# Decoder layer on one core: an SBUF tile moved into a pad, the last relu tiles placed in the u tiles, two down fetches on another queue, other tiles for the DMA adds

## The chip, the cores and the metric

The kernel runs on one core of a Trainium2 chip. A core has a matrix engine (TensorE, PE in the profile), a vector engine (VectorE, DVE), a scalar engine (ScalarE, ACT), GpSimd (POOL) and SyncE (SP). ACT, POOL and SP can each put DMA transfers in a queue of their own; every engine works through its instructions in program order and waits at semaphores. The metric is device time in microseconds; lower is better.

## The reference

One decoder layer, batch 1, 256 tokens, width 2048, all in float32:

```python
h   = rmsnorm(x, norm_attn_pre);  proj = h @ w_in          # 2048 x 4160
A   = dilated sliding-window attention, 8 heads x 128 (q, k, v from proj)
B   = latent attention, 8 heads (c_q @ w_uq, c_kv @ w_ukv, shared rotary key)
x   = x + rmsnorm(concat(A, B) @ w_out, norm_attn_post)    # 2048 x 2048
h   = rmsnorm(x, norm_mlp_pre)
u   = square(relu(h @ w_up))                               # 2048 x 8192
x   = x + rmsnorm(u @ w_down, norm_mlp_post)               # 8192 x 2048
```

## The kernel before

**Three passes.** Every float32 operand of a projection is split into a high part (ACT: a copy rounded to fp32r, line 311, or with a gain column, line 315) and a low part (DVE: value minus high part, lines 312 and 316). A product is then three fp32r matmuls, hi·hi, hi·lo and lo·hi (`three`, line 1083; all matmuls are recorded at line 301). The stationary operand is 128 tokens of the activation (xT, mixT, cqT, hT, u), the moving one up to 512 columns of a weight tile.

**Weights.** `Weights` streams the weights. SP loads a `raw` tile of 128 x 1024 (five buffers), ACT and DVE make `hi` and `lo` of it (eight buffers each), and `get` has tiles emitted six ahead of PE's use. What `weights.first[i]` holds is emitted just before tile i.

**Stages.** Input projections and attention; w_out; the up stage, chunk j = 0 to 7 of 1024 columns of w_up; the down stage, half c = 0 and c = 1 of 1024 columns of w_down, each over 64 row tiles k. Four k share one u tile g = k // 4.

**Pairs by seven products.** A pair of row tiles (2kp, 2kp + 1), with two blocks of 128 tokens and two halves of 512 columns, is a 2 x 2 x 2 block product. For the pairs in `DOWN_SEVEN[c]` (and three pairs in each up chunk but the first) it is done with seven block products in place of eight (`seven_products`, line 1088). For that, one fetch of 1 MB brings both weight tiles (`load_two`, line 378), DVE makes two sums of them (lines 366 to 371), and sums of the left operand are made and split (`st` in the up stage, `four_sums`, line 1040, and `s` tiles in the down stage). A fetch and its sums stand two weight tiles before the pair's first (`SUMS_AHEAD`). In the down stage the fetches alternate between the tile `ab_down` and the tile `c` (c = 0) or `u01` (c = 1), and all are issued by POOL. The products with sums go to accumulators m (up) and md (down); md is allocated at the first pair of a half. Left sums of pairs in both halves are written out (`keep_s`) and fetched back in c = 1.

**From up to down.** For each of u's 16 column tiles j of 512 and each token block b, `up_evac` (line 945) has ACT apply relu and square into a tile `r` (three buffers) and write it to DRAM (`rkeep`, by ACT's queue); 12 us later in the planner's time `turn_u` reloads it in another order (`x` or `c`, line 965, ACT's queue), and 8 us after that DVE transposes it in blocks into `uT[j]` (line 974). The tiles of u14 and u15 have the tag "T", two buffers that the sums of the up pairs used before. Planner's time is a clock that `Flow` advances by 0.216 us with every matmul of 512 columns it emits; it sets the order of the instructions only.

**Low parts of u.** `split_u` makes hi and lo of a u tile. For the tiles in `AWAY` the low part is made without DVE: ACT writes the negated high part to DRAM (`lo_away`, line 988), POOL issues two DMAs that add u to it (line 1000), and the sum is loaded as the low part (`load_lo`, line 1030, POOL). The adds of tiles 10 and up wait until the down stage has begun in the planner's time (`LATE`). The other low parts are written out in c = 0 (`keep_u`, SP's queue), and all but the first are loaded in c = 1.

**Addresses.** The allocator places tiles in steps of 32 bytes of a partition, from the left end (con, wp, then lat or hp, then dp) and from the right end (mix, pa, pb, up). Starts, in bytes of a partition:

| tiles | pool, side | start | remainder at 512 |
|---|---|---|---|
| con_pad, then the small tiles, pwn among them | con, left | 16512 | 128 |
| raw, hi, lo (weights) | wp, left | 18432 | 0 |
| hT_hi, hT_lo | hp, left | 104448, 120832 | 0 |
| ab_down, uhi, ulo, s | dp, left | 104448 and on | 0 |
| xT_hi, xT_lo | pa, right | 116704, 133088 | 480 |
| cqT | pb, right | 123872, 127968 | 480 |
| mixT_hi, mixT_lo | mix, right | 174560, 190944 | 480 |
| st, ab, ab2, c, u01, T, r, uT2 to uT9 | up, right | 139232 and on | 480 |

Slices of 128 tokens or 512 columns of a tile begin at multiples of 512 bytes. In the second half, the low parts of u tiles 4, 7, 8, 11, 12 and 15 lie in the up pool (line 1022).

Of the kernel before, what the change touches and what calls it, by code (L numbers as in the profile page):

```python
# [18 lines left out]
F32 = mybir.dt.float32  # L19
# [7 lines left out]
P = 128  # L27
D = 2048
S = 256
NB = S // P  # L30
# [15 lines left out]
CW = 1024  # L46
# [59 lines left out]
def up_steps(first, *groups):  # L106
    steps = [("k", k) for k in first]
    for i, ks in enumerate(groups):
# [8 lines left out]
N_SEVEN = [sum(w == "w" for w, _ in steps) for steps in UP_STEPS]  # L117


DOWN_SEVEN = ((9, 11, 13, 15, 19, 21, 23, 25, 27, 29), range(3, 28, 2))  # L120
AWAY = range(5, 14, 2)
LATE = 10
SHARED = [k for k in DOWN_SEVEN[0] if k in DOWN_SEVEN[1]]
GT = FF // 512
DOWN_STEPS = [[s for kp in range(2 * GT)
               for s in ([("w", kp)] if kp in ws else [("k", 2 * kp), ("k", 2 * kp + 1)])] for ws in DOWN_SEVEN]

# [141 lines left out]
def layer(nc, tc, io):  # L269
    flow = Flow()  # L270

    def pool(name, side, **kw):
        return tc.alloc_tile_pool(name=name, bufs=1, side=side, **kw)

    con = pool("con", "left")
    con.tile([P, 32], F32, name="con_pad")
    wp = pool("wp", "left")
    ps = tc.alloc_tile_pool(name="ps", bufs=1, space=PSUM)
    dram = tc.alloc_tile_pool(name="dram", bufs=1, space=bass.MemoryType.DRAM)
# [69 lines left out]
    late = {}  # L349

    def seven(load, targets):

        st, tt, H = {}, nc.vector.tensor_tensor, 512

        def fetch():
            ab = st["ab"] = load()
            st["a"], st["b"] = [ab[:, :CW], ab[:, CW:]] if not isinstance(ab, list) else ab

        def sums():
            ab, a, b = st["ab"], st["a"], st["b"]
            t, u = st["t"], st["u"] = targets()
            if not isinstance(ab, list):
                two = [x.rearrange("p (k n) -> p k n", n=H) for x in (t, ab)]
                tt(out=two[0], in0=two[1][:, 0:2, :], in1=two[1][:, 1:4:2, :], op=OP.add)
            else:
                for x, o in ((a, 0), (b, H)):
                    tt(out=t[:, o:o + H], in0=a[:, o:o + H], in1=x[:, H:], op=OP.add)
            tt(out=u[:, :H], in0=t[:, :H], in1=b[:, H:], op=OP.add)  # L370
            tt(out=u[:, H:], in0=u[:, :H], in1=b[:, :H], op=OP.add)  # L371

        def b11(hi, lo):
            split(hi[:, :H], lo[:, :H], st["a"][:, :H])

        return (fetch, sums), [b11] + [lambda hi, lo, n=n: split(hi, lo, st[n]) for n in "but"]

    def load_two(raw, queue, src):
        queue.dma_start(out=raw.rearrange("p (k n) -> p k n", k=2), in_=src.rearrange("(k p) n -> p k n", p=P))
        return raw  # L380
# [54 lines left out]
    def seven_down(c, kp):  # L435
        def load():

            n = DOWN_SEVEN[c].index(kp)
            raw = dpl["ab"]
            if n % 2:  # L440
                raw = late["u01" if c else "c"]
            return load_two(raw, nc.gpsimd, io["w_down"][2 * kp * P:(2 * kp + 2) * P, c * CW:(c + 1) * CW])

        return seven(load, lambda: [late["st"][:, i * CW:(i + 1) * CW] for i in range(2)])

    dpl, left, skeep, wide_d = {}, {}, {}, []
    for c in range(2):
        wide_d.append([])
        for what, k in DOWN_STEPS[c]:
            if what == "k":  # L450
                ts = [weights.plan(down_weight(c, k), 1, CW)]
            else:
                q, parts_q, back = [lambda c=c, k=k, f=f: f(c, k) for f in (down_sums, down_split, down_back)]
# [232 lines left out]
    for half in range(2):  # L686
        qkv = {}
        for nms in (("qk", "v") if not half else "qkv"):
            accs = [acc for _, _, acc in proj(xT, [ch_a[half, nms]], f"{nms}{half}",
                                              bank_of=at_bank if (half, nms) == (0, "v") else None)]  # L690
            for i, nm in enumerate(nms):
                t = pa.tile([P, NB, 512], F32, tag=nm, name=f"{nm}_{half}")
# [146 lines left out]

    pw, pwi = [con.tile([P, NB], F32, name=n) for n in ("pw", "pwi")]  # L840
    pws = con.tile([P, 4, NB], F32, name="pws")
    pwk, pwn = dram.tile([P, NB], F32, name="pwk"), con.tile([P, NB], F32, name="pwn")
    xkeep = [dram.tile([P, D], F32, name=f"xkeep{b}") for b in range(NB)]

    def by_quarter(rows):
# [69 lines left out]
    for ns in ((0, 1), (2,), (3,)):  # L915
# [4 lines left out]
        for c, b, acc in proj(mixT, [ch_o[n] for n in ns], f"o{ns[0]}", order, heads_done):  # L920
            n = ns[c]
# [20 lines left out]

    uT, ukeep = {}, {}

    def up_evac(j, b, acc, order):

        yield UP_STEP * order
        r = late["up"].tile([P, 512], F32, tag="r", bufs=3, name=f"r{j}_{b}")
        nc.scalar.activation(r, acc, AF.Relu, scale=rstd2[b])
        nc.scalar.activation(r, r, AF.Square)  # L950
        keep = dram.tile([P, 512], F32, name=f"rkeep{j}_{b}")
        nc.scalar.dma_start(out=keep.rearrange("(a t) (q c) -> (t q) a c", a=4, q=4),
                            in_=r.rearrange("m (a c) -> m a c", a=4))
        flow.start(turn_u(j, b, keep), D_BACK + (8.0 if (j, b) == (GT - 1, NB - 1) else 0.0))
# [3 lines left out]
    def turn_u(j, b, keep):  # L958

        o = 2 * b + j % 2  # L960
        if j < GT - 2:
            x = closing()[o]
        else:
            x = late["up"].tile([P, 512], F32, tag="r", bufs=3, name=f"x{j}_{b}")
        nc.scalar.dma_start(out=x, in_=keep)
        yield D_TURN
        if j not in uT:
            if j in (0, 1, 10, 11, 12, 13):
                t2 = late["u01" if j < 2 else "ab2" if j < 12 else "ab"][:, j % 2 * CW:(j % 2 + 1) * CW]
            else:  # L970
                tag = {"tag": "T", "bufs": 2} if j > 13 else {"tag": f"uT{j}", "bufs": 1}
                t2 = late["up"].tile([P, CW], F32, name=f"uT{j}", **tag)
            uT[j] = t2.rearrange("p (k s) -> p k s", k=4)
        nc.vector.transpose(uT[j][:, :, b * P:(b + 1) * P].rearrange("p k (q t) -> p k q t", q=4),
                            x.rearrange("p (q k c) -> p k q c", q=4, k=4))
        if b:
            turned.add(j)
            if j in AWAY:
                flow.start(lo_away(j), D_NEG)

    def lo_away(g):

        ukeep[g] = dram.tile([P, CW], F32, name=f"ukeep{g}")
        u = uT[g].rearrange("p k s -> p (k s)")
        for h in range(2):
            c = slice(h * 512, (h + 1) * 512)
            t = late["up"].tile([P, 512], F32, tag="r", bufs=3, name=f"neg{g}_{h}")
            nc.scalar.activation(t.bitcast(F32R), u[:, c], AF.Copy, scale=-1.0)
            yield 1.0
            nc.scalar.dma_start(out=ukeep[g][:, c], in_=t)  # L990
            yield D_LO
        if g < LATE:
            yield D_ADD
        else:
            while not dpl:
                yield 2.0
            yield 4.0 + 5.0 * (g % 2) + 20.0 * ((g - LATE) // 2)
        for h in range(2):
            c = slice(h * 512, (h + 1) * 512)
            nc.gpsimd.dma_start(out=ukeep[g][:, c], in_=u[:, c], accum_op=OP.add)  # L1000
            yield 2.0 if g < LATE else 10.0

    def split_u(c, g):
# [7 lines left out]
        u, h, l = [x.rearrange("p k s -> p (k s)") for x in (uT[g], uh, ul)]  # L1011
        if c and g or g in AWAY:
            nc.scalar.activation(h, u, AF.Copy)
# [18 lines left out]
    def keep_u(g):  # L1032
        ukeep[g] = dram.tile([P, CW], F32, name=f"ukeep{g}")
        nc.sync.dma_start(out=ukeep[g], in_=us[0, g][1].rearrange("p k s -> p (k s)").bitcast(F32))
# [78 lines left out]
    def closing():  # L1113
        return [late["c"][:, i * 512:(i + 1) * 512] for i in range(4)]
# [3 lines left out]
    for j in range(FF // CW):  # L1118
# [9 lines left out]
        for t, b in order:  # L1128
            what, k, tiles = steps[t]
# [14 lines left out]
            if what == "k":  # L1144
                w = weights.get(tiles[0])
                h_done(k, b)
                for n in range(2):
                    c = slice(n * 512, (n + 1) * 512)
                    three(accs[b, n], [tok(hT[x], k, b) for x in range(2)], [w[x][:, 0, c] for x in range(2)], t == 0, t == len(steps) - 1)
                    if j == 0 and t == len(steps) - 1:  # L1150
                        evac.append(flow.start(up_evac(n, b, accs[b, n], 0.75 * (2 * b + n))))
                    flow.pump()
                if b == NB - 1:
                    weights.free(tiles[0])
                continue
# [21 lines left out]
    up = late["up"]  # L1177
# [88 lines left out]
    for c in range(2):  # L1266
# [3 lines left out]
        accs = {(b, n): y[b][2 * c + n] for b, n in PARTS}  # L1270
        ws = DOWN_SEVEN[c]
        for t, (what, k, tiles) in enumerate(wide_d[c]):
            g = (2 * k if what == "w" else k) // 4
# [26 lines left out]
            if nxt not in us:  # L1300
                if not c and g > 1 and g - 1 not in AWAY:
                    keep_u(g - 1)
# [16 lines left out]
    for g in (GT - 2, GT - 1):  # L1319
        for b, n in PARTS:  # L1320
            for kk in range(4):
                k = 4 * g + kk
# [62 lines left out]
```

## Time and profile before

| | us |
|---|---|
| median of 3 runs | 1047.66 |
| lowest, highest | 1044.74, 1049.71 |
| the profiled execution | 1050.24 |
| its span, first to last instruction | 1048.5 |

The profile is of one execution. A row of the groups has line, engine, operation, out<-in, count, busy us, mean ns of one, and the idle time before them with what ended it. Matmul rows overlap each other (390 ns each at a distance of some 230), so the time of a run of matmuls is read from their starts. Half of the transfers' time is SP's queue:

```
q1 hardware_dynamic: 65200, 173.05, 49.9%
q0 software_dynamic: 16656, 59.78, 17.4%
q10 hardware_dynamic: 23376, 19.78, 5.8%
```

(q1 is SP's, q0 POOL's and q10 ACT's queue: packets, MB, share of 16 DMA engines.) The input stages run to about 359 us, the up stage to 699, the down stage to the end.

### The profile page before, as it was taken

To read this page: it belongs to the slowest core of one execution; us is meant where nothing else is said; L and a number is where in the kernel's file an instruction comes from. 1 tells how busy PE (TensorE), PEld (TensorE's weight loads), DVE (VectorE), ACT (ScalarE), POOL (GpSimd) and SP (SyncE) were. 2 spreads that over 40 slices of the span, in tenths; PEclk is the share of its full clock that TensorE was granted. 3 is DMA by queue.
4 is the path that set the end of the run, shared out by engine and by line. 5 is a ranking of instruction groups with operands and counts; after the bars stand their busy time and mean duration, and the time that the engine had idled before them with its cause. 6 is when DMAs were issued, how large, how long until landed. Compare 5 with 4: busy or idle time off the path is not lost.

```text
span 1048.5 us, 13268 instructions
## 1 busy us (share of the span) xinstructions
PE 1035.0 (99%) x4718; PEld 853.5 (81%) x4718; DVE 834.7 (80%) x1125; ACT 634.7 (61%) x850; POOL 64.1 (6%) x102
## 2 busy tenths in 40 slices
PE   9999999999999999999999999999999999999996
PEld 6888889889888878888888888887888888888885
DVE  6675536567547579999999999895899999998786
ACT  6674436556446467666676776675565666766561
POOL 0000000000001010000010100000101000211100
PEclk9999999999999999999999999998999999999999
DMA  8975547454437478877889878789869868888972
GB/s 293 371 221 152 139 131 224 149 163 148 144 130 240 140 287 286 265 243 226 275 253 306 274 225 290 214 280 333 286 243 354 294 211 316 290 306 301 318 267 81
DMA packets 105298, 253.44 MB, mean 242 GB/s; under 512 B 8720, under 2 KB 29712, under 8 KB 104848
## 3 DMA queue, kind: packets, MB, share of 16 engines
q1 hardware_dynamic: 65200, 173.05, 49.9%
q0 software_dynamic: 16656, 59.78, 17.4%
q10 hardware_dynamic: 23376, 19.78, 5.8%
q8 instruction: 37, 0.61, 0.2%
q14 instruction: 29, 0.24, 0.1%
HBM read 224.78 MB, written 27.79 MB: 241 GB/s over the span
## 4 chain that ended last, share of the span: by engine, by line
PE 76%; DVE 10%; issue 6%; DMA 5%; ACT 2%; POOL 1%; ACTq 0%; DVEq 0%; POOLq 0%; SPq 0%
PE acc_u L301 22%; PE y L301 13%; PE acc_o L301 8%; PE m L301 5%; PE acc_qk L301 4%; DVE lo L312 4%; PE acc_v L301 4%; PE md L301 3%; PE acc_ckv L301 2%; PE acc_q L301 2%; PE acc_k L301 2%; PE acc_cq L301 2%; PE acc_ukv L301 2%; PE acc_uq L301 2%; DMA ab_down<-in_w_down 1%
## 5 line engine op out<-in xcount | busy, mean ns | idle before, releaser
L312 DVE TENSOR_TENSOR lo<-raw,hi 128x1024 fp32r<-128x1024 f32 (+3 forms) x207 | 234.0, 1150 | 95.2 <-ACT hi L311 94.4
L311 ACT ACTIVATE hi<-raw 128x1024 fp32r<-128x1024 f32 (+3 forms) x207 | 203.3, 996 | 72.6 <-DMA raw<-in_w_down 15.9
L301 PE MATMUL acc_u<-hi,hT_lo 128*128 128x512 f32 x386 | 150.6, 390 | 0.4 <-DVE hT_lo L312 0.4
L301 PE MATMUL acc_u<-hi,hT_hi 128*128 128x512 f32 x386 | 150.9, 391 | 0.0
L301 PE MATMUL acc_u<-lo,hT_hi 128*128 128x512 f32 x386 | 150.2, 389 | 0.0
L301 PE MATMUL y<-hi,uhi 128*128 128x512 f32 x358 | 140.7, 393 | 2.3 <-ACT uhi L311 2.3
L301 PE MATMUL y<-lo,uhi 128*128 128x512 f32 x358 | 141.0, 394 | 0.4 <-DVE lo L312 0.4
L301 PE MATMUL y<-hi,ulo 128*128 128x512 f32 x358 | 140.8, 393 | 0.6 <-DVE ulo L312 0.6
L315 ACT ACTIVATE hi<-raw,gcol 128x1024 fp32r<-128x1024 f32 x86 | 96.8, 1148 | 31.8 <-PE acc_u L301 12.5
L316 DVE SCALAR_TENSOR_TENSOR lo<-raw,gcol,hi 128x1024 fp32r<-128x1024 f32 x86 | 106.8, 1275 | 9.9 <-ACT hi L315 9.8
L301 PEld LDWEIGHTS acc_u<-hi,hT_lo 128*128 128x128 f32 x386 | 72.4, 188 | 16.0 <-DVE hT_lo L312 0.9
L301 PEld LDWEIGHTS acc_u<-hi,hT_hi 128*128 128x128 f32 x386 | 72.5, 188 | 15.1
L301 PEld LDWEIGHTS acc_u<-lo,hT_hi 128*128 128x128 f32 x386 | 72.5, 188 | 15.0
L301 PEld LDWEIGHTS y<-hi,uhi 128*128 128x128 f32 x358 | 67.9, 190 | 17.2 <-ACT uhi L311 2.7
L301 PEld LDWEIGHTS y<-hi,ulo 128*128 128x128 f32 x358 | 67.9, 190 | 15.7 <-DVE ulo L312 1.7
L301 PEld LDWEIGHTS y<-lo,uhi 128*128 128x128 f32 x358 | 67.9, 190 | 15.5 <-DVE lo L312 1.1
L312 DVE TENSOR_TENSOR lo<-st_down,hi 128x1024 fp32r<-128x1024 f32 x46 | 55.1, 1221 | 0.8 <-ACT hi L311 0.8
L301 PE MATMUL acc_o<-hi,mixT_hi 128*128 128x512 f32 x128 | 52.4, 410 | 0.0
L311 ACT ACTIVATE hi<-st_down 128x1024 fp32r<-128x1024 f32 x46 | 47.9, 1053 | 5.0 <-DVE st_down L371 3.6
L301 PE MATMUL acc_o<-hi,mixT_lo 128*128 128x512 f32 x128 | 50.7, 396 | 0.0
L301 PE MATMUL acc_o<-lo,mixT_hi 128*128 128x512 f32 x128 | 50.5, 395 | 0.0
L311 ACT ACTIVATE hi<-u 128x1024 fp32r<-128x1024 f32 (+1 forms) x33 | 32.4, 982 | 29.5 <-PE y L301 12.3
(336 smaller groups left out, 2027.0 us busy)
## 6 DMA issues: line engine op xcount, KB each, us to landing
raw<-in_w_up SPq DMA_DIRECT2D x86, 512.0 KB, 4.9
raw<-in_w_down SPq DMA_DIRECT2D x82, 512.0 KB, 6.2
raw<-in_w_in SPq DMA_DIRECT2D x55, 512.0 KB, 4.9
ab<-in_w_up POOLq DMA_DIRECT2D x17, 1024.0 KB, 7.2
raw<-in_w_out SPq DMA_DIRECT2D x32, 512.0 KB, 4.5
ab_down<-in_w_down POOLq DMA_DIRECT2D x12, 1024.0 KB, 9.0
ulo<-ukeep POOLq DMA_DIRECT2D x20, 512.0 KB, 6.4
rkeep<-r ACTq DMA_DIRECT2D x32, 256.0 KB, 3.4
```

Of the source, the lines that this page charges most:

```text
L301: nc.tensor.matmul(out, a, b, start=start, stop=stop)
L311: nc.scalar.activation(hi, src, AF.Copy)
L312: nc.vector.tensor_tensor(out=lo, in0=src, in1=hi.bitcast(F32), op=OP.subtract)
L315: nc.scalar.activation(hi, src, AF.Copy, scale=g)
L316: nc.vector.scalar_tensor_tensor(out=lo, in0=src, scalar=g, in1=hi.bitcast(F32), op0=OP.mult, op1=OP.subtract)
```

## The change

- `con_pad`, a tile of 128 bytes that nothing used, is named `spare_con`, and pwn (8 bytes, a step of 32) is a view of it. con is 32 bytes shorter; wp begins at 18400, and hp and dp at 104416.
- `up_evac` of u14 and u15 writes relu and square into the u tile itself, half b of it, in place of an r tile. `u_tile` makes the tile on first use.
- In c = 0 the pairs are 7, 9, 11, 13, 15, 19, 21, 23, 27, 29 (25 left out, 7 added). 25 is then no longer shared by the halves, and 7 is.
- The first two of these (7 and 9) are fetched by SP, into ab_down and c.
- `AWAY` is 3, 5, 7, 9, 11 in place of 5, 7, 9, 11, 13; of tiles 10 and up, only 11 is in it, and its adds stand 55 us of planner's time after the down stage's begin (9 and 29 us before, for 11 and 13).

```diff
-DOWN_SEVEN = ((9, 11, 13, 15, 19, 21, 23, 25, 27, 29), range(3, 28, 2))
-AWAY = range(5, 14, 2)
+DOWN_SEVEN = ((7, 9, 11, 13, 15, 19, 21, 23, 27, 29), range(3, 28, 2))
+AWAY = range(3, 12, 2)
...
-    con.tile([P, 32], F32, name="con_pad")
+    spare_con = con.tile([P, 32], F32, name="spare_con")
...
-            return load_two(raw, nc.gpsimd, io["w_down"][2 * kp * P:(2 * kp + 2) * P, c * CW:(c + 1) * CW])
+            return load_two(raw, nc.gpsimd if c or n > 1 else nc.sync, io["w_down"][2 * kp * P:(2 * kp + 2) * P, c * CW:(c + 1) * CW])
...
-    pwk, pwn = dram.tile([P, NB], F32, name="pwk"), con.tile([P, NB], F32, name="pwn")
+    pwk, pwn = dram.tile([P, NB], F32, name="pwk"), spare_con[:, :NB]
...
+    def u_tile(j):
+        if j not in uT:
+            if j in (0, 1, 10, 11, 12, 13):
+                t2 = late["u01" if j < 2 else "ab2" if j < 12 else "ab"][:, j % 2 * CW:(j % 2 + 1) * CW]
+            else:
+                tag = {"tag": "T", "bufs": 2} if j > 13 else {"tag": f"uT{j}", "bufs": 1}
+                t2 = late["up"].tile([P, CW], F32, name=f"uT{j}", **tag)
+            uT[j] = t2.rearrange("p (k s) -> p k s", k=4)
+        return uT[j]
+
     def up_evac(j, b, acc, order):
 
         yield UP_STEP * order
-        r = late["up"].tile([P, 512], F32, tag="r", bufs=3, name=f"r{j}_{b}")
+        if j < GT - 2:
+            r = late["up"].tile([P, 512], F32, tag="r", bufs=3, name=f"r{j}_{b}")
+        else:
+            r = u_tile(j)[:, 2 * b:2 * b + 2, :].rearrange("p k s -> p (k s)")
         nc.scalar.activation(r, acc, AF.Relu, scale=rstd2[b])
...
-        if j not in uT:
...
-        nc.vector.transpose(uT[j][:, :, b * P:(b + 1) * P].rearrange("p k (q t) -> p k q t", q=4),
+        nc.vector.transpose(u_tile(j)[:, :, b * P:(b + 1) * P].rearrange("p k (q t) -> p k q t", q=4),
...
-            yield 4.0 + 5.0 * (g % 2) + 20.0 * ((g - LATE) // 2)
+            yield 55.0
```

More of the change, by code (lines that the diff above doesn't have):

```diff
@@ L966, in turn_u @@
         yield D_TURN
-        if j not in uT:
[L968 to L973, printed above, removed]
-        nc.vector.transpose(uT[j][:, :, b * P:(b + 1) * P].rearrange("p k (q t) -> p k q t", q=4),
+        nc.vector.transpose(u_tile(j)[:, :, b * P:(b + 1) * P].rearrange("p k (q t) -> p k q t", q=4),
                             x.rearrange("p (q k c) -> p k q c", q=4, k=4))
```

## The prediction

> **What bounds the kernel now.** The page first: is one engine the bound, and where does it pause?
>
> ```profile
> span 1048.5 us, 13268 instructions
> PE 1035.0 (99%) x4718; PEld 853.5 (81%) x4718; DVE 834.7 (80%) x1125; ACT 634.7 (61%) x850; POOL 64.1 (6%) x102
> ...
> PEclk9999999999999999999999999998999999999999
> ...
> L301 PE MATMUL acc_u<-hi,hT_lo 128*128 128x512 f32 x386 | 150.6, 390 | 0.4 <-DVE hT_lo L312 0.4
> ...
> L301 PE MATMUL y<-hi,uhi 128*128 128x512 f32 x358 | 140.7, 393 | 2.3 <-ACT uhi L311 2.3
> ```
>
> PE is busy 99% of the span, so only two things can shorten it: the time from one matmul to the next (the pitch; the 390 ns of a row overlap), and the few pauses, one of which shows as the single 8 in PEclk. The pitch stands in the chain of waits in order of time (start, us, what):
>
> ```profile
> 50.92 22.40 PE acc_v L301 x96
> ...
> 151.65 3.20 PE acc_ckv L301 x24
> ...
> 375.80 44.91 PE acc_u L301 x198
> ...
> 904.49 5.44 PE y L301 x24
> ...
> 914.69 5.55 PE y L301 x24
> ```
>
> acc_v takes 22.40 / 96 = 233.3 ns, acc_u 44.91 / 198 = 226.8, y 226.7 in one block and 231.3 in another, all of 512 columns. What differs is addresses. By remainder at 512 bytes, the weights (moving, pool wp) stand at 0; of the stationary tiles hT and those of dp stand at 0, and xT, mixT, cqT, st and the second half's low parts in the up pool at 480. Equal remainders give 226.7, unequal ones 233.3. One stage has both, PE's timeline in chunk 1:
>
> ```profile
> 424.00 0.40 PE L301 MATMUL m<-hi,st 128*128 128x512 f32 x1
> ...
> 424.70 0.39 PE L301 MATMUL m<-hi,hT_hi 128*128 128x512 f32 x1
> ...
> 425.38 0.39 PE L301 MATMUL acc_u<-hi,hT_hi 128*128 128x512 f32 x1
> ```
>
> Three matmuls from st take 0.70 us, the three from hT that follow at once, into the same tile, 0.68: no stage or engine is to blame. The pause stands in the busy time by stretches (us, PE busy (x count), then PEld, DVE, ACT, POOL; PEclk, DMA share, GB/s):
>
> ```profile
> 699.00:732.00 33.00, 30.47 (x120) 24.15 (x119) 20.70 (x24) 19.43 (x23) 2.34 (x3) 0.90 0.93 321
> 732.00:754.00 22.00, 22.00 (x99) 18.21 (x98) 20.41 (x25) 11.02 (x12) 2.19 (x3) 1.00 0.89 289
> 754.00:850.00 96.00, 96.00 (x426) 79.47 (x425) 90.04 (x110) 60.96 (x70) 7.88 (x12) 1.00 0.85 297
> ```
>
> 120 matmuls at 0.2267 are 27.2 us; the stretch took 33.0, so the start of the down stage loses **5.8 us**. ACT's and PE's timelines show how:
>
> ```profile
> 706.87 0.37 ACTq L952 DMA_DIRECT2D rkeep<-r  x1
> 707.86 1.06 ACT L311 ACTIVATE hi<-raw 128x1024 fp32r<-128x1024 f32 x1 [1.03 <-PE y L301]
> 716.33 0.69 ACT L949 ACTIVATE r<-acc_u,rstd_pre 128x512 f32<-128x512 f32 x1 [7.40 <-DMA rkeep<-r]
> ```
> ```profile
> 720.52 0.39 PE L301 MATMUL y<-hi,ulo 128*128 128x512 f32 x1
> 723.21 0.80 PE L301 MATMUL y<-hi,uhi 128*128 128x512 f32 x1 [2.30 <-ACT uhi L311]
> ...
> 725.25 0.63 PE L301 MATMUL y<-hi,uhi 128*128 128x512 f32 x1
> ...
> 729.51 0.63 PE L301 MATMUL y<-lo,uhi 128*128 128x512 f32 x1
> ```
>
> The third of the last four relus (u14, b = 1) needs one of three r buffers and waits 7.40 us until an earlier rkeep write has read that one. Behind it in ACT's order stand the hi parts of the next weights; DVE's lo parts follow them; PE runs dry at 720.5 for 2.3 us, and ten matmuls from 725.25 to 729.51 run at 0.426 each, half speed. The write shares the DMA engines with two fetches of POOL's (its timeline; then rows of the DMA view, 699 to 720: issues, KB, median us to landing):
>
> ```profile
> 699.45 0.73 POOL L379 DMA_DIRECT2D ab_down<-in_w_down  x1 [32.98 <-PE acc_u L301]
> ...
> 705.81 1.03 POOL L379 DMA_DIRECT2D c<-in_w_down  x1
> ```
> ```profile
> c<-in_w_down POOLq DMA_DIRECT2D x1, 1024.0 KB, 12.8
> rkeep<-r ACTq DMA_DIRECT2D x3, 256.0 KB, 12.3
> ```
>
> **The change part by part.** (1) pwn moves into the pad. con shrinks by one step of 32 bytes, so wp, hp and dp slide from remainder 0 to 480: every fp32r matmul then has both operands at 480. Unequal now, and equal after, are the groups
>
> ```profile
> L301 PE MATMUL acc_o<-hi,mixT_hi 128*128 128x512 f32 x128 | 52.4, 410 | 0.0
> ...
> L301 PE MATMUL m<-hi,st 128*128 128x512 f32 x84 | 33.2, 396 | 0.0
> ...
> L301 PE MATMUL acc_qk<-hi,xT_hi 128*128 128x512 f32 x64 | 25.9, 405 | 0.3 <-ACT hi L311 0.3
> ...
> L301 PE MATMUL acc_v<-hi,xT_hi 128*128 128x512 f32 x64 | 25.3, 395 | 0.0
> ...
> L301 PE MATMUL acc_q<-hi,xT_hi 128*128 128x512 f32 x32 | 13.6, 426 | 0.0
> ```
>
> each of the projections three times (three passes), and acc_k, acc_cq and acc_ukv like acc_q: (128 + 64 + 64 + 4 x 32) x 3 = 1152 matmuls x 6.6 ns = 7.6 us. st: 84 + 42 of m and 63 of acc_u, 189 x 6.6 = 1.2. The low parts of the second half in the up pool, 71 matmuls, each with the one before it (5.55 against 5.44 with eight of them, so 14 ns apiece): 1.0. Sum **-9.8 us**, all on PE, which waits for little else there. No matmul of this trace has both operands at 480, so the new pitch is bounded: below by 0.213 (the half-speed rows halved: streaming alone), above by 0.240 (6.6 more for each operand off 0). I take 0.2267, the row of equal remainders. For it speaks acc_ckv, unequal but of 288 columns: 133.3 ns, 13.3 over 288/512 of 0.213, and 13.3 is what equal tiles of 512 columns pay. The stationary tile's own address costs nothing there; so what costs is how the two reads meet. DVE and ACT are not touched by the shift: lo from st_down, in the up pool, takes what lo from raw takes (first rows):
>
> ```profile
> L312 DVE TENSOR_TENSOR lo<-raw,hi 128x1024 fp32r<-128x1024 f32 x19 | 22.8, 1220 | 0.0
> L312 DVE TENSOR_TENSOR lo<-st_down,hi 128x1024 fp32r<-128x1024 f32 x16 | 19.5, 1222 | 0.3 <-ACT hi L311 0.3
> ...
> L366 DVE TENSOR_TENSOR st_down<-ab_down 128x1024 f32<-128x1024 f32 x4 | 4.9, 1223 | 0.1
> L370 DVE TENSOR_TENSOR st_down<-st_down,ab_down 128x512 f32<-128x512 f32 x4 | 2.8, 693 | 0.1
> ```
>
> (2) The last four relus write into the T tiles of u14 and u15, whose earlier readers, the splits of the last up sums, have to be done before the last up products can run. The 7.40 us wait goes: **-5.8 us**, if nothing is late next. Next in ACT's order come the four reloads of x, which wait for the same rkeep writes to land; they stand 12 us of the planner's time later, against landings of about 12 in this stretch. The transposes of u14 and u15 now also wait for the write of b = 1, whose half they overwrite; they come 15 us after it. Both fit, with little to spare; the ends are 0 and the 5.8 given back.
>
> (3) The fetches of the first two down pairs go from POOL to SP and stand there between raw loads, which costs SP two issues. The first follows the raw load of k = 11, the second that of k = 13.
>
> ```profile
> 705.31 0.33 SPq L195 DMA_DIRECT2D raw<-in_w_down  x1
> ```
> ```profile
> L301 PE MATMUL y<-hi,ulo x358: 388/389/794, 699.4 to 1028.8; 128*128 128x512 f32 x179
> ...
> L1030 POOL DMA_DIRECT2D ulo<-ukeep x20: 528/536/561, 749.1 to 998.9; - x20
> ...
> DMA to landing us min/median/max: 2.7/6.2/11.4
> ```
>
> That load is k = 11's, so the fetch goes out near 706, not at 699.45, and no longer beside the first rkeep. Behind its landing wait DVE's sums of pair 7 and, behind them, the lo parts from k = 12 on. Landing by 719 (the 12.8 above), sums 1.22 + 2 x 0.69 = 2.6, lo 1.2: 723. PE, 12 x 0.2267 = 2.72 us per k from 699, wants k = 12 at 732. Hidden by 9 us; without that cover each further us of landing is a us of PE. On POOL the load of g = 3's low part and the fetch of pair 11, wanted 50 us on, move up.
>
> (4) Ten pairs as before, 7 for 25, so PE's work is the same; its first half of down starts the pairs four tiles earlier. DVE's work from 699 to 850 is the same too, in 6 us less: its idle time there is 33.0 - 20.7, 22.0 - 20.4 and 96 - 90.0, together 19.9 us, 12.3 of it where pair 7's sums now come. Nothing. In the second half pair 7's left sums come back by DMA, and pair 25's are made on DVE: alike.
>
> (5) The DMA adds for g = 3 in place of 13 take two negations and their writes out of ACT's crowded stretch (1.2 us of ACT, not counted) into the up stage, where those of 5, 7, 9 and 11 are hidden already (the acc_u row above has 0.4 us of waits). g = 3's low part is loaded once k = 7 frees its buffer, 10.9 us before k = 12 wants it, against 6.2 us, 11.4 at worst (rows above): nothing, or half a us. The 55 us for g = 11 place its adds later on POOL; they are wanted at g = 10.
>
> Sum: -9.8 - 5.8 = -15.6 on the profiled execution's 1050.24 us (span 1048.5 and 1.7 around it): 1034.6. The median of the runs is 1047.66, 2.6 lower; from it, **1032**.
>
> **Rivals.** *A new wait at the start of down:* the x reloads on ACT, or DVE's sums on a fetch that lands over 20 us after its issue. PE pauses again, 3 to 5.8 us: 1035 to 1038. *The pitch stays as it is in each stage, and only (2) counts:* 1041.9. The st and hT rows of one stage speak against it. [...] *Slower: the stationary tile's own address decides.* Then hT and dp's tiles become slow and xT gains nothing: 3 x (386 + 358) matmuls of the first rows and some 400 from m, md and s, 2630 x 6.6 = 17.4 us, 1047.7 - 5.8 + 17.4 = 1059.3; if the moving one pays as well, near 1086. It decides as soon as 512 columns stream beside a load off 0, from the up stage on. acc_ckv speaks against it; for it, that no row has both operands off 0. *Better than equal:* towards 0.213, as low as 980.
>
> **Numbers.** Forecast 0.64, new wait 0.15, pitch as it is 0.08, slower 0.10, better 0.03. The range 1026 to 1043 holds the first three with the runs' spread. A measurement of this kernel tells about 0.5%, 5.2 us: faster 0.85, same 0.05, slower 0.10.
>
> **What would show it.** acc_v x96 at 21.8 us; m from st and from hT both 0.68 for three; acc_u and y still at 0.2267 (0.233 or more if I am wrong); no wait of ACT for rkeep at the relus, no 8 in PEclk, md 38 us after the first y; no long DVE wait for the fetch of pair 7. A stall that only moves to the x reloads would show as ACT waiting for rkeep in the L965 loads.

## The result and the profile after

The changed kernel takes 1036.34 us (median of 4 runs, 1034.94 to 1037.25) against 1048.68 of the kernel before (4 runs, 1044.74 to 1052.21): a ratio of 0.9882, with a 95% interval of 0.9844 to 0.9921, or 12.3 us less. The profiled execution took 1035.85 us with a span of 1034.1, 14.4 less than the span before.

The page of the changed kernel (span; PE's busy time; the granted clock in 40 slices; the chain of waits by engine; one group with its idle time behind the second bar):

```profile
span 1034.1 us, 13262 instructions
...
PE 1022.4 (99%) x4718; PEld 851.3 (82%) x4718; DVE 834.4 (81%) x1125; ACT 634.6 (61%) x850; POOL 63.5 (6%) x100
...
PEclk9999999999999999999999999999999999999998
...
PE 96%; DVE 1%; DMA 1%; issue 1%; ACT 0%; POOL 0%; DVEq 0%; POOLq 0%; SPq 0%; ACTq 0%
...
L301 PE MATMUL y<-hi,uhi 128*128 128x512 f32 x358 | 139.3, 389 | 0.0
```

The share of PE is 99% as before, and that says little: the work became shorter and the pauses went. The only 8 left in the clock is in the last slice, where PE runs out of work; y has no idle time (2.3 us before), and PE makes 96% of the chain (76% before). Its pieces in order of time (start, length, count) give the pitch:

```profile
50.95 21.76 PE acc_v L301 x96
...
290.20 5.49 PE acc_o L301 x24
...
371.27 44.92 PE acc_u L301 x198
...
692.95 38.08 PE y L301 x168
```

acc_v is at 21.76 / 96 = 226.7 ns (233.3 before), acc_u and y stay at 226.9 and 226.7; acc_o is at 228.8, not quite there. In one stage, three matmuls from st and the three from hT behind them now both take 0.68 us (PE's timeline in chunk 1):

```profile
419.43 0.39 PE L301 MATMUL m<-hi,st 128*128 128x512 f32 x1
...
420.11 0.39 PE L301 MATMUL m<-hi,hT_hi 128*128 128x512 f32 x1
...
420.79 0.39 PE L301 MATMUL acc_u<-hi,hT_hi 128*128 128x512 f32 x1
```

The other signs that were named came too: the first md starts 38.1 us after the first y (55.1 before), ACT has no wait at the last relus, and DVE's longest wait from 690 to 740 us is 1.6 us, for ACT and not for the fetch of pair 7. The busy time by stretches, shifted by the 6.2 us that the down stage now begins earlier:

```profile
692.80:726.00 33.20, 33.20 (x148) 27.52 (x147) 28.85 (x36) 23.07 (x28) 1.26 (x2) 1.00 0.95 331
726.00:748.00 22.00, 22.00 (x99) 18.23 (x98) 21.66 (x28) 12.65 (x15) 2.90 (x4) 1.00 0.99 352
748.00:844.00 96.00, 96.00 (x426) 79.50 (x425) 92.95 (x107) 62.13 (x70) 6.83 (x10) 1.00 0.83 293
```

In the first 33 us PE now does 148 matmuls where it did 120, at full clock. DVE has 4.4 + 0.3 + 3.1 = 7.7 us of idle time left in the three stretches, of 19.9 before.

**Where the 14.4 us come from.** The first y starts at 692.78 us in place of 698.98, the last at 1025.08 in place of 1039.85. So 6.2 us are gained before the down stage and 8.6 in it (0.4 are given back around them). To split the 8.6, take all distances between the starts of neighbouring matmuls that are over 0.3 us and add up what each has above 0.227. Between 685 and 740 us that is 6.0 us in the kernel before and nothing after; from 740 to the last y it is 1.4 and nothing. What is left, 1.2 us, is put down to the pitch of the low parts in the up pool.

### The profile page after: what moved, and what is told of

Its sections match the earlier page's. It is cut to its first block, busy times and chain, and to the rows that moved or that the text cites. A ratio compares the mean times of both kernels' runs of the same rounds, so it can differ in the third digit from the quotient of the medians.

```text
span 1034.1 us, 13262 instructions
## 1 busy us (share of the span) xinstructions
PE 1022.4 (99%) x4718; PEld 851.3 (82%) x4718; DVE 834.4 (81%) x1125; ACT 634.6 (61%) x850; POOL 63.5 (6%) x100
## 4 chain that ended last, share of the span: by engine, by line
PE 96%; DVE 1%; DMA 1%; issue 1%; ACT 0%; POOL 0%; DVEq 0%; POOLq 0%; SPq 0%; ACTq 0%
PE acc_u L301 26%; PE y L301 25%; PE acc_o L301 8%; PE md L301 6%; PE m L301 6%; PE acc_v L301 4%; PE acc_qk L301 4%; PE acc_ckv L301 2%; PE acc_ukv L301 2%; PE acc_q L301 2%; PE acc_cq L301 2%; PE acc_k L301 2%; PE acc_uq L301 2%; PE sc_b L301 1%; DMA raw<-in_w_in 1%
```

## The experiments

Twelve kernels, in three sets on three occasions, each set with its own runs of the kernel before (their medians: 1050.99, 1050.29 and 1051.76 us). "Lost" is the sum just explained, from one profiled execution of each kernel. e4, with one execution, is not in the table.

| kernel | edits in it | median us | ratio, 95% | first y at | lost 685 to 740 | lost later |
|---|---|---|---|---|---|---|
| before | none | 1048.68 | 1 | 698.98 | 6.0 | 1.4 |
| after | all five | 1036.34 | 0.9882 (0.9844 to 0.9921) | 692.78 | 0.0 | 0.0 |
| e1 | address | 1044.57 | 0.9928 (0.9901 to 0.9955) | 693.00 | 5.9 | 3.1 |
| e2 | all but address | 1044.66 | 0.9937 (0.9916 to 0.9958) | 699.36 | 0.0 | 1.4 |
| e3 | relu tiles | 1045.91 | 0.9951 (0.9934 to 0.9967) | 698.71 | 0.5 | 0.9 |
| e5 | address, all at 0 | 1040.78 | 0.9904 (0.9876 to 0.9932) | 692.98 | 1.3 | 2.3 |
| e6 | all but relu tiles | 1038.65 | 0.9887 (0.9867 to 0.9908) | 691.32 | 0.0 | 2.4 |
| e7 | all but SP fetch | 1035.28 | 0.9858 (0.9837 to 0.9879) | 692.71 | 0.0 | 1.0 |
| e9 | address, relu tiles | 1038.12 | 0.9885 (0.9861 to 0.9909) | 691.87 | 6.8 | 2.2 |
| e11 | address, adds | 1041.87 | 0.9916 (0.9885 to 0.9948) | 691.44 | 0.3 | 5.1 |
| e12 | address, pairs | 1046.31 | 0.9950 (0.9934 to 0.9966) | 692.21 | 10.4 | 1.1 |
| e13 | address, SP fetch | 1037.81 | 0.9877 (0.9850 to 0.9904) | 691.97 | 1.4 | 1.6 |
| e14 | address, pairs, adds | 1037.11 | 0.9868 (0.9841 to 0.9895) | 692.47 | 0.0 | 1.5 |

One execution doesn't tell how often the stall occurs, but every execution has its mean granted clock on record. In the profiled execution of the kernel before it is 0.995, with half the clock for 6.8 us behind the stall; in that of the changed kernel it is 0.997, with half the clock only at the end. The 38 executions of the kernel before in the three sets fall into two groups: 33 at 0.997 or below (all but one of them at 0.996 or below) took 1049.2 to 1053.5 us, and five at 0.998 or above took 1043.5 to 1046.8. Executions at 0.996 or below are five of six of e1, two of four of e5, two of six of e9 and all nine of e12, and none of the 43 of the changed kernel, e2, e3, e6, e7, e11, e13 and e14. So, where no edit prevents it, the long stall occurs in some executions and not in others, and the "lost" of one execution is not the mean of its kernel.

### The two main terms alone (e1, e2, e3)

e1, the kernel before with the address alone:

```diff
-    con.tile([P, 32], F32, name="con_pad")
+    spare_con = con.tile([P, 32], F32, name="spare_con")
...
-    pwk, pwn = dram.tile([P, NB], F32, name="pwk"), con.tile([P, NB], F32, name="pwn")
+    pwk, pwn = dram.tile([P, NB], F32, name="pwk"), spare_con[:, :NB]
```

> Only pwn in the pad; wp, hp and dp slide to remainder 480. Theory (equal remainders at 512 give the short pitch): acc_v x96 in 21.8 us, three m from st in 0.68, the first y some 6 us earlier; ACT's wait of 7 us at the relus and PE's pause of 5.8 us stay; 1048.7 - 7 = about 1041.5. Rival (addresses do nothing, all of the gain is at the start of down): acc_v 22.4, 1048.7.

The ACT timeline of e1 at the last relus (start, length, instruction, in brackets the idle time before it and what ended it):

```profile
702.91 0.69 ACT L949 ACTIVATE r<-acc_u,rstd_pre 128x512 f32<-128x512 f32 x1 [2.73 <-DMA ukeep<-neg]
...
708.37 0.69 ACT L949 ACTIVATE r<-acc_u,rstd_pre 128x512 f32<-128x512 f32 x1 [1.90 <-DMA rkeep<-r]
...
714.11 0.69 ACT L949 ACTIVATE r<-acc_u,rstd_pre 128x512 f32<-128x512 f32 x1 [2.82 <-DMA rkeep<-r]
```

6.0 us are gained up to the first y and none in the down stage. The stall is there, but its waits are spread over three relus, and the first of them waits for a write of `neg`: the r ring is shared. Three kinds of tiles take their turn in its three buffers, the relus, the negated high parts of u13 (`lo_away`) and the x reloads.

e2, the changed kernel with pwn back in con:

```diff
-    spare_con = con.tile([P, 32], F32, name="spare_con")
+    con.tile([P, 32], F32, name="con_pad")
...
-    pwk, pwn = dram.tile([P, NB], F32, name="pwk"), spare_con[:, :NB]
+    pwk, pwn = dram.tile([P, NB], F32, name="pwk"), con.tile([P, NB], F32, name="pwn")
```

> The changed kernel with pwn back in con, so that the weights stand at remainder 0 again. Theory: acc_v x96 back at 22.4 us, no pause at the start of down; 1036.3 + 6 to 7 = about 1043. Rival (addresses do nothing): 1036.

Nothing is gained before the first y and no stall is left at the start of down: the two halves of the gain are independent, and 0.9928 x 0.9937 = 0.9865 is within the interval of the whole.

e3, the kernel before with `u_tile` and the new lines of `up_evac` alone:

```diff
-        r = late["up"].tile([P, 512], F32, tag="r", bufs=3, name=f"r{j}_{b}")
+        if j < GT - 2:
+            r = late["up"].tile([P, 512], F32, tag="r", bufs=3, name=f"r{j}_{b}")
+        else:
+            r = u_tile(j)[:, 2 * b:2 * b + 2, :].rearrange("p k s -> p (k s)")
```

> The kernel before with the last four relus in the u tiles, nothing else. Theory (the r buffers make the wait): no wait of ACT at the relus, PE pauses less than 1 us between 699 and 732, 1048.7 - 6 = about 1043. Rival (POOL's two fetches delay the rkeep writes, and ACT then waits at the x reloads instead): PE pauses 3 us or more, 1045 to 1049.

Waits of ACT from 690 to 735 us in e3 (us in total, times, longest):

```profile
ACT hi L311 <- DMA rkeep<-uT: 5.6, 1, 5.6
```

No wait is left at the relus. The one that is next, at an x reload, is 5.6 us long and costs PE only 0.5, likely because by then the weights are split further ahead; no run tests this reason. None of the ten executions has the drop of the clock. So the relu tiles alone do what the prediction said of them, 0.9951.

### Which addresses count (e4, e5)

e4 is the changed kernel with pads of other lengths (and a pad at the front of hp and of dp), so that the stationary tiles stand at these distances from the weights' remainder, in bytes: xT +32, mixT -256, hT +64, dp +128, cqT -128, st 0.

```diff
-    mix.tile([P, 64], F32, name="mix_pad")
+    mix.tile([P, 128], F32, name="mix_pad")
...
-    pa.tile([P, 104], F32, name="pa_pad")
+    pa.tile([P, 32], F32, name="pa_pad")
...
-    pb.tile([P, 104], F32, name="pb_pad")
+    pb.tile([P, 72], F32, name="pb_pad")
...
+    hp.tile([P, 16], F32, name="hp_pad")
...
+    dp.tile([P, 32], F32, name="dp_pad")
```

> The changed kernel with pads that set the stationary tiles off from the weights' 480: xT by +32, mixT by -256, hT by +64, the tiles of dp by +128, cqT by -128 bytes; st stays equal. Theory (remainder at 512): acc_v, acc_o, acc_u and y all near 233 ns a matmul, m from st 226.7; about 1036 + 3800 x 6.6 ns = 1061. Rival (only lines of 64 bytes count): acc_v 233, acc_o, acc_u and y 226.7; about 1039. Second rival (226.7 is no floor): one of the offsets comes below 226.

One execution, 1055.97 us. Its chain of waits:

```profile
51.12 22.40 PE acc_v L301 x96
...
304.95 49.95 PE acc_o L301 x219
373.72 46.20 PE acc_u L301 x198
704.13 38.79 PE y L301 x168
747.81 5.57 PE y L301 x24
```

acc_v (+32) is at 233.3 ns, acc_u (+64) at 46.20 / 198 = 233.3, and acc_o (-256) at 228.1, as in the changed kernel, whose piece of 219 of acc_o takes 49.95 as well. A distance of 256 bytes is as good as none; 32 and 64 cost the same 6.6 ns. y (+128) is at 230.9 and 232.1, so 128 bytes cost somewhat less, 4 to 5 ns, and the whole kernel comes to less than the 1061 expected. Nothing comes below 226. One expectation failed: st keeps the weights' remainder, but its matmuls of m stand 226 to 233 ns apart here, next to matmuls from hT, and no run says why. The matmuls from cqT (-128) have 384 columns and give no clear reading.

e5, the kernel before with 480 bytes left free at the right end, so that all these tiles stand at remainder 0:

```diff
     wp = pool("wp", "left")
+    rp = pool("rp", "right")
+    rp.tile([P, 120], F32, name="right_pad")
```

> The kernel before with 480 bytes left free at the right end, so that the pools of the right side slide from remainder 480 to 0 and meet the weights and hT there; nothing else is changed. Theory (the two operands only have to be equal): xT, mixT, cqT and st fall from 233.3 to 226.7 ns just as they do with all at 480; the first y comes 6 us before that of the kernel before, the stall at the start of the down stage stays, and the time is that of the change of addresses alone, 0.993 of the kernel before, 1043 to 1045. Rival (480 itself is the good address): 233 ns stay in the input stages and the time is that of the kernel before, ratio 1.000.

```profile
51.10 21.76 PE acc_v L303 x96
...
371.47 44.91 PE acc_u L303 x198
```

The chain of e5 (line 303 is line 301 of the others) has the same pitch as that of the changed kernel, and the first y comes at 692.98, as in e1. The remainder 480 is nothing special. The median was lower than expected (1040.78, expected 1043 to 1045). Two of the four executions have the drop of the clock (1042.23 and 1042.78 us), two have not (1037.46 and 1039.33); the one profiled is the last of these, with 1.3 us lost. It is a mixture of both kinds, and so few executions don't show that it has the stall less often than e1.

### What makes the stall (e6, e7, e9)

The first theory was the prediction's: the r buffers make it, the queue of the fetch doesn't matter, the pairs and adds are worth nothing. e6 is the changed kernel with the edit of e3 taken back; in e7 POOL fetches the first two pairs of the changed kernel; e9 is the kernel before with the edits of e1 and e3.

```diff
-            return load_two(raw, nc.gpsimd if c or n > 1 else nc.sync, io["w_down"][2 * kp * P:(2 * kp + 2) * P, c * CW:(c + 1) * CW])
+            return load_two(raw, nc.gpsimd, io["w_down"][2 * kp * P:(2 * kp + 2) * P, c * CW:(c + 1) * CW])
```

(This is the whole of e7's edit.)

> The changed kernel with the last four relus in the r buffers again. Theory (the third of the four needs a buffer that an rkeep write still reads): ACT waits for rkeep at the relu, 4 us or more, PE pauses 2 to 4 us behind it and runs at half its clock for 2 to 3 us after: the down stage gives back 4 to 6 us, 1040 to 1042, 0.992 to 0.994 of the kernel before. Rival (the two fetches on POOL's queue slowed the write, and SP's later fetches have taken that away): no wait of ACT above 1.5 us, the time of the changed kernel, 1036 to 1037, 0.988.

> The changed kernel with the first two down pairs fetched by POOL again. Theory (the fetch was hidden on either queue): 1036 to 1037.5, 0.988 to 0.990 of the kernel before, and no pause of PE above 0.6 us at the start of the down stage. Rival (a fetch beside the first rkeep makes the x reloads on ACT wait, and the weights behind them): ACT waits 5 us or more at a reload, PE pauses 1 to 3 us, 1038 to 1041.

> The kernel before with two edits of the five alone: pwn in the pad, and the last relu tiles in the u tiles. Theory (the two carry all the gain, and the other three are worth nothing): first y 6 us earlier, down stage 6 to 8 us shorter, 1035.5 to 1037.5, 0.988 to 0.990 of the kernel before. Rival (the pairs, the DMA adds and the queue take away the two short pauses of the down stage, 0.8 and 0.6 us, and the wait at the x reloads): 1038 to 1040, 0.990 to 0.992, with pauses of PE near 845 and 980.

e6 has the waits of its rival. The last two relus in ACT's timeline of e6, in r buffers again:

```profile
700.92 0.67 ACT L949 ACTIVATE r<-acc_u,rstd_pre 128x512 f32<-128x512 f32 x1
...
703.76 0.67 ACT L949 ACTIVATE r<-acc_u,rstd_pre 128x512 f32<-128x512 f32 x1
```

They have no idle time before them, PE loses nothing here, and none of the six executions has the drop of the clock. So the other edits remove the stall by themselves. But the rival's reason, the queue, is not it either: e7 puts the fetches back on POOL's queue and has no stall, at 1035.28 us. And e9, with the two edits that should carry all the gain, has a median of 1038.12 us, but the execution that was profiled (1043.71, the longest of six) has a stall of 6.8 us without a wait for a transfer at the relus. One more of the six has the drop of the clock (1041.60); the other four took 1037.06 to 1038.51. ACT's waits from 690 to 735 us in e9, and the transfer rates of its DMA view from 685 to 735 (40 slices of 1.25 us):

```profile
ACT hi L311 <- DMA raw<-in_w_down: 10.2, 4, 8.6
```
```profile
GB/s 288 311 259 311 252 206 387 193 213 187 239 395 410 413 422 385 408 390 315 323 368 408 411 353 406 403 405 413 385 386 302 156 269 218 175 34 349 213 298 390
```

This time it was a raw tile that came late, by 8.6 us, behind a stretch (from about 699 us on) in which the DMA engines moved 302 to 422 GB/s, some 390 on average. In that stretch stand two fetches of 1 MB for pairs that are wanted some 50 us later, the rkeep writes, 13's negated writes and its add, and the raw loads wanted at once. The new theory, which the next set was to test: this stretch is overloaded, and whichever transfer is late stops ACT; the relu tiles take one waiter away, the other edits take transfers out of the stretch.

### One edit at a time beside the address (e11 to e14)

```diff
-AWAY = range(5, 14, 2)
+AWAY = range(3, 12, 2)
...
-            yield 4.0 + 5.0 * (g % 2) + 20.0 * ((g - LATE) // 2)
+            yield 55.0
```
```diff
-DOWN_SEVEN = ((9, 11, 13, 15, 19, 21, 23, 25, 27, 29), range(3, 28, 2))
+DOWN_SEVEN = ((7, 9, 11, 13, 15, 19, 21, 23, 27, 29), range(3, 28, 2))
```
```diff
-            return load_two(raw, nc.gpsimd, io["w_down"][2 * kp * P:(2 * kp + 2) * P, c * CW:(c + 1) * CW])
+            return load_two(raw, nc.gpsimd if c or n > 1 else nc.sync, io["w_down"][2 * kp * P:(2 * kp + 2) * P, c * CW:(c + 1) * CW])
```

The first is added to e1 in e11, the second in e12, the third in e13, the first two in e14.

> The kernel before with pwn in the pad, and the DMA adds for tiles 3, 5, 7, 9 and 11, those of 11 later, in place of 5 to 13; relus in r, pairs and queue as before. Theory (the stall is made by transfers: from 699 to 720 us the DMA engines are full, and 13's two negated writes and its add are among them): ACT waits under 4 us at the relus, PE pauses under 1.5 us, 0.989 to 0.991 of the kernel before, 1038 to 1041. Rival (the third r buffer alone makes the stall, or the pairs and the queue took it away): as with the addresses alone, a wait of 4.5 us or more and a pause of 3 us, 0.9925 to 0.994, 1043 to 1045.

> The kernel before with pwn in the pad, and pairs 7, 9, 11 ... 29 in the first half in place of 9, 11 ... 25 ... 29; relus, DMA adds and queue as before. Theory (the pair that is fetched first is now wanted 15 us after its fetch and not 50, so that it stands for two raw loads that are wanted just then, 1 MB less in the full stretch): a pause of PE under 1.5 us at the start of down, 0.989 to 0.991, 1038 to 1041. Rival (the adds or the r buffer): a wait of ACT of 4.5 us or more, a pause of 3 us, 0.9925 to 0.994, 1043 to 1045.

> The kernel before with pwn in the pad, and the first two down pairs fetched by SP; relus, pairs and DMA adds as before. Theory (the fetches go out later and behind raw loads, but their bytes stay in the full stretch): the pause shrinks little, 0.991 to 0.993, 1041 to 1043. Rival (the fetch that POOL issues 0 to 7 us before the rkeep writes is what slows them): no pause above 1 us, 0.988 to 0.990, 1037 to 1040.

> The kernel before with pwn in the pad, the new pairs and the new DMA adds; the relus in r and the fetches on POOL as before, so of the changed kernel only two edits are missing. Theory (the stall goes when the transfers of the stretch get fewer, so the relu tiles are a second cure of the same stall and add little): 0.988 to 0.9895, 1037 to 1039, no pause of PE above 1.5 us. Rival (the relu tiles or SP's queue are needed): 0.991 to 0.994, 1041 to 1044, ACT waiting 4 us or more at the relus.

**e12: the pairs alone don't cure it**, against the theory's expectation and beyond its rival's; the profiled execution loses more than that of e1, though the intervals of the two medians overlap. POOL's timeline, ACT's waits (690 to 740 us), a row of the DMA view (692 to 720; the last number is the median of us from issue to landing) and PE's timeline:

```profile
692.67 0.73 POOL L379 DMA_DIRECT2D ab_down<-in_w_down  x1 [39.57 <-PE acc_u L301]
693.40 0.91 POOL L1000 DMA_DIRECT2D ukeep<-ab  x1
697.94 0.74 POOL L379 DMA_DIRECT2D c<-in_w_down  x1 [3.63 <-ACT r L950]
705.25 0.86 POOL L1000 DMA_DIRECT2D ukeep<-ab  x1 [6.57 <-DMA ukeep<-neg]
```
```profile
ACT r L949 <- DMA rkeep<-r: 6.5, 1, 6.5
...
ACT r L949 <- DMA ukeep<-neg: 4.9, 1, 4.9
```
```profile
raw<-in_w_down SPq DMA_DIRECT2D x7, 512.0 KB, 12.0
```
```profile
721.41 0.80 PE L301 MATMUL y<-hi,uhi 128*128 128x512 f32 x1 [7.28 <-ACT uhi L311]
```

With pair 7 first, the second fetch leaves at 697.94 us, in e1 at 703.94. Both fetches and both adds now fall on the relus, raw loads take 12.0 us, ACT waits 11.4 us at the relus, PE 7.3 us.

**e14: the adds beside them cure it.** POOL's timeline and the same row of the DMA view:

```profile
692.93 0.71 POOL L379 DMA_DIRECT2D ab_down<-in_w_down  x1 [63.70 <-PE acc_u L301]
714.70 0.56 POOL L1030 DMA_DIRECT2D ulo<-ukeep  x1 [21.05 <-DVE st_down L366]
715.24 0.70 POOL L379 DMA_DIRECT2D c<-in_w_down  x1
```
```profile
raw<-in_w_down SPq DMA_DIRECT2D x10, 512.0 KB, 6.3
```

The load of g = 3's low part waits on POOL until 714.70 and holds the second fetch back behind it; 13's writes are gone from ACT's queue and from the r ring. Raw loads land in 6.3 us, and relus in r buffers wait 1.0 us in all. Which of the two, the later fetch or the freer ring, does more was not separated.

**e11: the adds without the pairs** hold back both fetches.

```profile
713.66 0.56 POOL L1030 DMA_DIRECT2D ulo<-ukeep  x1 [85.52 <-DVE st_down L1046]
714.21 0.72 POOL L379 DMA_DIRECT2D ab_down<-in_w_down  x1
714.91 0.74 POOL L379 DMA_DIRECT2D c<-in_w_down  x1
```

No stall at the relus (0.3 us lost), but 5.1 us lost later, in pauses of up to 1.5 us between 757 and 998: 1041.87 us. ACT's longest wait from 690 to 740 us, PE's waits for y, and the stretch from 720 to 740 (after PEld stands DVE):

```profile
ACT hi L311 <- DMA ab_down<-in_w_down: 8.0, 1, 8.0
```
```profile
PE y L301 <- DVE lo L312: 2.1, 3, 1.3
...
PE y L301 <- DVE ulo L312: 1.1, 2, 0.6
```
```profile
720.00:740.00 20.00, 20.00 (x88) 16.23 (x87) 11.94 (x17) 6.25 (x8) 2.21 (x3) 1.00 0.74 274
```

Now the fetch is late: ACT waits 8.0 us for it, DVE behind it is idle for 8 of 20 us, and the later pauses all end on DVE. That DVE lacks later what it didn't do here is likely, but no run tells it apart.

**e13: SP's queue alone** removes most of the stall, where the theory said little. SP's timeline in e13:

```profile
714.69 0.43 SPq L379 DMA_DIRECT2D ab_down<-in_w_down  x1
...
719.83 0.38 SPq L379 DMA_DIRECT2D c<-in_w_down  x1
```

Behind the raw loads the two fetches leave 16 to 21 us later than POOL sends them in e1 (693.47 and 703.94), after the rkeep writes. A wait of 4.0 us at one relu stays, 1.4 us are lost, and the time is 1037.81 us. e13 changes the queue and the time of the fetches together, so which of the two counts is not separated. In the changed kernel and in e6, SP's first fetch leaves at 700.21 and 698.82 us, among the rkeep writes, and there is no stall either.

Of all versions e7 (1035.28 us), e14 and the changed kernel have the shortest medians, and their intervals overlap: none is shown to beat the others.

**What this leaves of the theory.** The stretch is as full without the stall as with it. From 690 to 730 us, e1 and then e7 (last two numbers: DMA share, GB/s):

```profile
690.00:730.00 40.00, 36.20 (x151) 29.17 (x151) 27.27 (x32) 24.98 (x30) 2.34 (x3) 0.96 0.97 332
690.00:730.00 40.00, 40.00 (x178) 33.14 (x177) 33.33 (x42) 26.06 (x31) 2.69 (x4) 1.00 0.99 357
```

e7 moves more and PE has no pause there, so a full stretch alone doesn't make the stall. A second reading fits the kernels with relus in r buffers as well: where the negated tiles of u13 share the ring (before, e1, e5, e12, e13), the last relus wait 3.2 to 11.4 us in all for writes that still read a buffer; where the new adds have taken u13 out of the ring (e6, e11, e14), they wait 1.0 us at most. It doesn't explain e9, whose relus are not in the ring and whose late tile is raw. No run changed the ring alone, by a fourth buffer say, or the traffic alone, so what makes a transfer late enough to stop PE stays open. What is shown is which edits keep the drop of the clock away: the new adds in every kernel that has them, SP's fetch beside the address (e13, 1.4 us still lost), and the relu tiles in all ten executions of e3, but only in four of six of e9.

## Why the prediction was right, and where it was not

The range and the sign held; the time came out 4.3 us above the forecast of 1032 and the profiled execution 1.2 us above the sum (1035.85 against 1034.64). The 1.2 us hide two larger errors. Of the 14.4 us between the two profiled executions, the addresses gave 6.2 and 1.2 in place of 9.8, and the stall 6.0 in place of 5.8; 1.4 came from short pauses after 740 us that stand in no term of the sum, and 0.4 were given back. That these 1.4 made up for more than half of what the addresses lacked is luck.

- **What bounds the kernel.** As read: pitch and one stall, and the short pauses beside them. The address alone and all but the address (e1, e2) multiply to the whole.
- **(1) The addresses.** The mechanism holds: 233.3 became 226.7 where it was said, acc_u and y kept theirs, and the rivals "as it is in each stage" and "the stationary tile's own address" fell; "better than equal" did too, since no pitch came below 226. The assumption that no row could show, that both at 480 are as good as both at 0, holds too (e5). The size was too large. Of 8.8 us before the down stage (1152 and 189 matmuls at 6.6 ns), 6.2 came; the ten profiles with equal addresses in the table have their first y at 692.3 on average, the three with unequal ones at 699.0, 6.7 less. The term that was mis-sized is "1152 matmuls x 6.6", and the step that failed is that PE "waits for little else there": acc_qk's 192 gave nothing in the changed kernel (its last matmul starts at 50.57 us, at 50.53 before) and up to 1.5 us in the others (e6), since this stage runs behind the first weights, PE's waits in the changed kernel:

```profile
PE acc_qk L301 <- ACT hi L311: 1.3, 3, 0.6
```

And acc_o came down to 228.1 to 228.8, with 1.8 us gained of 2.5; acc_q, acc_k, acc_cq and acc_ukv stand at 228.4 to 229.2 on average and not at 226.7. The low parts of the second half gave 1.2 of the 1.0 said.
- **(2) The stall.** The proximate wait was read rightly, and the relu tiles alone take it away in the kernel before (e3: 0.5 us lost in place of 6.0). The price holds for the profiled execution: 6.0 against 5.8. But the step "the 7.40 us wait goes: -5.8 us" gave the whole stall to the r buffers. They are not enough to explain it: e6 has no stall with the relus in r, two of six executions of e9 have one without, and SP's fetch, or the adds, keep it away as well. And it is not in every execution: five of 38 of the kernel before have no drop of the clock, so one execution doesn't price it for the median.
- **(3), (4), (5) "Nothing".** Not so one at a time. Beside the address alone (0.9928) SP's fetch gives 0.9877; the pairs give 0.9950, with an interval that still overlaps but a loss of 10.4 us in the profile; the adds take the loss at the relus away and bring another of 5.1 us later in the profile (0.9916). What failed is that each was costed on its own waits and engine, not by what it does to the other waits in these 20 us: which tiles share the r ring, and which transfers go at the same time. That the DMA engines have no room there shows in the stretch 710 to 720 of the kernel before (last but one number: DMA share),

```profile
710.00:720.00 10.00, 10.00 (x46) 8.28 (x45) 0.91 (x2) 3.07 (x4) 0.00 (x0) 1.00 1.02 356
```

and the prediction took only landing times from it. With (2) done the sum of the three is near nothing: 0.9885 in e9 against 0.9882 for all five, and 0.9951 in e3 against 0.9937 in e2, with intervals that overlap.
- **The rivals.** "A new wait at the x reloads": in the changed kernel ACT does wait there, 3.43 us at 713.91,

```profile
713.91 1.06 ACT L311 ACTIVATE hi<-raw 128x1024 fp32r<-128x1024 f32 x1 [3.43 <-DMA rkeep<-uT]
```

and PE doesn't feel it: the cover that the prediction counted on held.
- **How the number was put together.** The 15.6 us were worked out on an execution 2.6 us above the median of three and then taken in full from that median. One of the three took 1044.74 us, which by its time is likely one without the stall. In the larger sets the median of the kernel before is 1050.3 to 1051.8, so the profiled execution was the ordinary one, and the step down by 2.6 is the largest part of the 4.3 us; the sum itself, 1034.6, is 1.7 below the measured median.

The rates in this stretch: the slices of e9 above from 699 to 722 us show 302 to 422 GB/s; what the DMA engines can move at most was not measured. That a transfer there is late for want of bandwidth is not shown, since e7 moves 357 GB/s from 690 to 730 us, at a DMA share of 0.99, and nothing stops.

## What to carry to other kernels

A stall that ends in a wait for a write may go away by edits that don't touch the waiting instruction: before a wait is priced, list what else moves in the same stretch and which tiles share its buffers. Edits that look free, since their own waits are hidden, are priced by what they do to the other waits of such a stretch, and several cures of one stall don't add up. A stall that comes and goes is priced from many executions, and their granted clocks tell which of them had it. And a kernel of back-to-back fp32r matmuls is worth a look at its tiles' addresses: equal remainders at 256 bytes for the stationary and the moving tile gave 6.6 ns per matmul of 512 columns here.

## What was not expected of the hardware

- Equal remainders at 256 bytes are enough (e4: acc_o at -256 takes 228.1 ns, as it does at 0 in the changed kernel), and the price doesn't grow with the distance: 32 and 64 bytes give 233.3 ns both, 128 bytes 231 to 232.
- PE's clock fell to half behind a pause of 2.69 us. Measured from start to start, this one (before, at 720.5) ended in a matmul that already ran at half the clock (the granted clock is 0.50 from 723.2 to 729.9 us), and so did the ones up to 729.5, 0.426 us each. The longest pauses of e1, e9 and e12 (3.5, 3.2 and 7.7 us) were followed by such a drop too (granted clock 0.96, 0.97 and 0.87 from 690 to 730 us), while pauses up to 2.11 us in these traces left the clock full. The longest of those is in e5, up to 997 us (its stretch 980 to 1010, with the clock third from the end):

```profile
980.00:1010.00 30.00, 28.23 (x124) 22.73 (x123) 24.87 (x25) 17.38 (x19) 1.59 (x3) 1.00 0.83 274
```

  The two slow starts behind the 2.69 us (0.6 and 0.85 us) come after the drop and are no part of that pause. No run varied the length of a pause alone.
- The same instructions don't always stall. The profiled executions of e1 and e5, which differ only in where their tiles lie, lost 5.9 and 1.3 us at the same place; the six executions of e9 spread from 1037.06 to 1043.71 us, and their granted clocks (0.998 in the four short ones, 0.996 and 0.995 in the two long ones) say that the drop of the clock makes the difference. That the order in which transfers land differs from one execution to the next would explain it; only one execution of each kernel has a trace, so no run shows it.
